# Two SBUF slots 1088 instead of 1032 columns wide: the same program at other addresses

## The chip, the cores and the metric

The kernel runs on one core of a Trainium2 chip. The metric is the device time of one execution in microseconds, taken as the median of three runs. A profile is one further execution with the hardware profiler on. Five engines work side by side and wait for each other by semaphores: PE (TensorE, the matmuls; its weight loads stand in rows of their own as PEld), DVE (VectorE), ACT (ScalarE), POOL (GpSimd) and SP (SyncE), which here issues nearly all DMAs.

## The reference

Two decoder layers over 1024 tokens of 1024 features, all in float32. What is computed, cut to its products:

```python
# layer 0: mLSTM, 8 heads, in chunks
q, k, v, o, ig, fg = split(rmsnorm(x) @ w_in)          # 1024 -> 512, 512, 1024, 1024, 8, 8
h = mlstm(q, k, v, ig, fg)                              # chunk by chunk: scores, values, carried state
x = x + rmsnorm((headnorm(h) * sigmoid(o)) @ w_out)
x = x + rmsnorm(conv_ffn(rmsnorm(x)))                   # in both layers
# layer 1: attention with a forget gate, 16 heads, K and V projected once
k, v, f = split(rmsnorm(x) @ kv_w);  q, g = split(rmsnorm(x) @ w_qg)
x = x + rmsnorm((attend(q, k, v, cumsum(logsigmoid(f))) * sigmoid(g)) @ w_out)

def conv_ffn(h):                                        # D_FF = 2816
    y = causal_conv3(h @ w_up)                          # 1024 -> 2 * 2816
    gate, val = split(y)
    return (gelu(gate) * val) @ w_down                  # 2816 -> 1024
```

## The kernel before

**Precision.** A product of two float32 matrices is made of three passes in a faster type (`fp32r`): each operand is split into a high part and a rest, and high x high, high x rest and rest x high are summed in PSUM. Line 196 (ACT) writes the high part, line 197 (DVE) the rest. So each product takes three matmuls, and PE carries almost all of the time.

**What a matmul reads.** `matmul(out, st, mv)` loads the stationary operand `st` (128 columns) into the array and streams the moving operand `mv` (512 or 256 columns) past it. Both lie in SBUF. A row of the profile for line 779 reads `b<-x,s`: the output is a PSUM bank `b`, the moving operand lies in `x`, the stationary one in a slot `s`.

**Where the operands lie.** `x` is one SBUF tile of 64 KB per partition with the split activations. All else lies in numbered slots of one pool (`Core.slot`, below), as a rule 1024 float32 columns (4096 bytes per partition) wide, or in pairs of slots that share one tile of 2048 columns: `p0` to `p5` (`PAIRS`). A few slots are wider (`WIDE`): six hold up to 4 x 272 columns of weights, and slots 2 and 31 hold 8 x 129 columns (the values of eight heads with a column of ones, the carried state). The pool lays the tiles one behind the other in the order of their first use, and `x` and the constants behind them. The mLSTM stage uses the same slots by other numbers (`renamed`).

**The stages, in order.** The mLSTM layer (until 522 us in the profile): projections of v (line 282, 256 or 272 moving columns, `gi` 0 to 3 are four column blocks), of k and q (line 282 by way of `proj_T`, 512 columns, four pairs `p` of heads each), of the gate o (256 columns), the recurrence, and the output projection (line 301). Then the first FFN: the up projection (line 779, 522 to 975 us) and the down projection (line 933, to 1188 us). Then the attention layer (to 1900 us; its projections lines 282, 1167 and 1183, scores line 1319, values line 1346, output line 301), and the second FFN (up to 2352 us, down to the end).

**The up projection** forms 22 blocks `f`. Each `f` has seven products (Strassen-like sums of blocks), and each product is 12 matmuls of 512 columns in one uninterrupted run: 84 matmuls per `f`. The moving operand of the products 11, 12, S3 and 22 is `x`, that of S2, S1 and S4 a pair of tiles `p`. The stationary weights lie here (`RIGHT` maps products to these):

```python
UP = {"11": ((18, 0), (18, 512)), "21": ((0, 0), (0, 512)), "T2": ((1, 0), (2, 0)), "T1": ((1, 512), (2, 512)),
      "T3": ((3, 0), (4, 0)), "T4": ((3, 512), (4, 512)), "22": ((5, 0), (5, 512))}
```

So product 11 takes slot 18, product 12 slot 0, S2 and S1 slots 1 and 2, S3 and 22 slots 3 and 4, S4 slot 5. In the profile a run of `b<-x,s` x36 is product 22 of one `f` with 11 and 12 of the next, x24 of `b<-p,s` is S2 and S1, then come x12 for S3 and x12 for S4.

**The down projection** copies both operands, split, into `x`, and multiplies out of `x` alone.

**The other places that the prediction names.** In the mLSTM stage, q of pairs p = 0, 1 has its weights in slots 0, 27, 1, 30, q of pairs 2, 3 in halves of `p3` and `p4`, k of pairs 2, 3 in slots 14, 32 and `p5`. Of the 256-column products, v of `gi` 3 has its (moving) weights in slots 0, 1, 27, 30, and the first o block in slots 14, 32 and `p5`.

The order of the work is the program's. In PE's long stretches it is written out by hand. It does not depend on how wide a slot is.

Of the kernel before, what the change touches and what calls it, by code (L numbers as in the profile page):

```python
# [34 lines left out]
SLACK = 0, 20  # L35
PIECES = {5: (8, 20, 26, 32, 38), 10: (6, 8, 17, 21, 25, 29, 33, 37, 41, 45)}

WIDE = {0: 1088, 1: 1088, 15: 1088, 27: 1088, 29: 1088, 30: 1088, 2: 1032, 31: 1032}
PAIRS = (19, 22), (20, 21), (23, 24), (25, 12), (26, 13), (28, 17)
PAIR = {i: (j, n) for j, two in enumerate(PAIRS) for n, i in enumerate(two)}  # L40
BLOCK = {(0, 0): 0, (0, 1): 1, (1, 1): 2, (1, 0): 3}
# [7 lines left out]
class Core:  # L49
# [30 lines left out]
    def slot(self, i, dt):  # L80
# [3 lines left out]
        if self.slots.get(key, (None, None))[1] != dt:  # L84
            n, name = (WIDE.get(i, 1024), key) if half is None else (2048, f"p{key}")
            self.slots[key] = self.arena.tile([P, n], dt, tag=name, name=name), dt
# [1499 lines left out]
```

## Time and profile before

| | us |
|---|---|
| median of three runs (2573.05 to 2577.49) | 2576.5 |
| profiled execution, its own time | 2575.71 |
| span of the profile, first to last instruction | 2574.0 |
| PE busy | 2465.4 |
| DVE busy | 1571.4 |
| ACT busy | 1167.4 |
| POOL busy | 639.6 |

The span is 1.7 us shorter than the execution's time. Matmuls overlap: a row's mean of one is how long a matmul is under way, not how often one starts. The pace of PE is read from starts: the start of one run of matmuls to the start of the next, divided by the matmuls between. All paces here were read at a granted clock of 1.00 (2.4 GHz).

### The profile page before, as it was taken

How to read it: one execution, taken by the hardware profiler on the slowest of the kernel's cores; microseconds unless marked ns; L12 is line 12 of the kernel's file. 1: busy time of each engine (PE TensorE's matmuls, PEld its weight loads, DVE VectorE, ACT ScalarE, POOL GpSimd, SP SyncE). 2: the span in 40 equal slices, each digit the busy share in tenths (PEclk: the TensorE clock that was granted, in tenths of full speed). 3: DMA queues.
4: the chain of work that ended last, by engine and by line, in shares of the span. 5: the costliest groups of instructions: out<-in, count | busy, mean ns of one | idle time of the engine just before them, and what ended most of it. 6: DMA issues, size and time to landing. Idle time of an engine off the chain costs nothing. (4 is left out here: it accounts for less than half of the span.)

```text
span 2574.0 us, 34090 instructions
## 1 busy us (share of the span) xinstructions
PE 2465.4 (96%) x12552; PEld 2047.9 (80%) x12552; DVE 1571.4 (61%) x2442; ACT 1167.4 (45%) x2078; POOL 639.6 (25%) x545
## 2 busy tenths in 40 slices
PE   7999996989999999998999999999989999999998
PEld 7988785867888888877888888887767888888886
DVE  6312544666766769558465555556776676678746
ACT  5212333344544554347255555555434454454434
POOL 0000110034454441001133333223023545442000
PEclk9999997999999999999999999999999999999999
DMA  7434333223233247443655544553332323327443
GB/s 217 117 115 139 101 90 103 90 74 106 90 115 101 88 146 263 140 140 125 195 145 137 162 132 142 156 141 119 111 102 82 103 88 116 100 90 277 144 130 128
DMA packets 291795, 332.04 MB, mean 129 GB/s; under 512 B 21036, under 2 KB 208268, under 8 KB 291628
## 3 DMA queue, kind: packets, MB, share of 16 engines
q1 hardware_dynamic: 291052, 328.82, 41.1%
q8 instruction: 98, 1.61, 0.3%
q10 hardware_dynamic: 576, 1.05, 0.1%
q14 instruction: 69, 0.57, 0.1%
HBM read 230.03 MB, written 99.78 MB: 128 GB/s over the span
## 5 line engine op out<-in xcount | busy, mean ns | idle before, releaser
L779 PE MATMUL b<-x,s 128*128 128x512 f32 x2112 | 510.8, 396 | 9.9 <-ACT s L196 5.0
L779 PEld LDWEIGHTS b<-x,s 128*128 128x128 f32 x2112 | 397.6, 189 | 107.8 <-ACT s L196 5.8
L196 ACT CAST s<-s 128x1024 fp32r<-128x1024 f32 (+3 forms) x319 | 230.5, 728 | 423.2 <-PE b L779 350.5
L197 DVE TENSOR_TENSOR s<-s,s 128x512 fp32r<-128x512 f32 (+3 forms) x312 | 282.0, 908 | 209.1 <-ACT s L196 203.6
L779 PE MATMUL b<-p,s 128*128 128x512 f32 x1584 | 389.6, 400 | 10.5 <-ACT s L787 10.4
L779 PEld LDWEIGHTS b<-p,s 128*128 128x128 f32 x1584 | 301.9, 191 | 83.9 <-ACT s L787 12.1
L933 PE MATMUL b<-x 128*128 128x512 f32 x1452 | 336.0, 389 | 1.5 <-DVE x L197 1.5
L933 PEld LDWEIGHTS b<-x 128*128 128x128 f32 x1452 | 272.4, 188 | 59.0 <-DVE x L197 2.4
L796 DVE SCALAR_TENSOR_TENSOR s<-s,cp,s 128x1023 f32<-128x1023 f32 (+1 forms) x176 | 241.0, 1372 | 28.4 <-ACT s L794 26.7
L1167 PE MATMUL b<-x,s 128*128 128x512 f32 x816 | 240.1, 411 | 0.0
L196 ACT CAST x<-s 128x1024 fp32r<-128x1024 f32 (+2 forms) x144 | 128.6, 918 | 230.8 <-PE b L933 176.9
L197 DVE TENSOR_TENSOR x<-s,x 128x1024 fp32r<-128x1024 f32 (+2 forms) x144 | 152.2, 1078 | 118.4 <-ACT x L196 117.7
L1326 POOL TENSOR_SCALAR p<-p,ring 128x256 f32<-128x256 f32 (+7 forms) x128 | 99.6, 781 | 318.4 <-DVE ring L1325 304.1
L757 POOL TENSOR_TENSOR s<-s,s 128x512 f32<-128x512 f32 x44 | 91.2, 2072 | 321.5 <-issue 198.0
L1167 PEld LDWEIGHTS b<-x,s 128*128 128x128 f32 x816 | 148.1, 190 | 24.2
L785 DVE TENSOR_TENSOR s<-s,b 128x512 f32<-128x512 f32 x132 | 90.3, 684 | 111.5 <-PE b L779 111.5
L754 POOL TENSOR_TENSOR s<-s,s 128x512 f32<-128x512 f32 x44 | 59.7, 1357 | 361.5 <-DVE ring L189 225.0
L794 ACT ACTIVATE s<-s,cp 128x1024 f32<-128x1024 f32 x88 | 109.4, 1246 | 32.0 <-DVE s L785 13.4
L197 DVE TENSOR_TENSOR p<-b,p 128x512 fp32r<-128x512 f32 x162 | 91.1, 580 | 49.5 <-ACT p L196 49.1
L196 ACT CAST p<-b 128x512 fp32r<-128x512 f32 (+2 forms) x178 | 87.9, 511 | 68.9 <-PE b L1334 46.3
L787 ACT COPY s<-b 128x512 f32<-128x512 f32 x176 | 102.3, 581 | 34.4 <-PE b L779 32.9
L282 PE MATMUL two<-s,x 128*128 128x256 f32 (+1 forms) x768 | 107.9, 289 | 10.0 <-DVE F L1131 7.8
(282 smaller groups left out, 4005.5 us busy)
## 6 DMA issues: line engine op xcount, KB each, us to landing
s<-in_ffn_w_up_dram SPq DMA_DIRECT2D x176, 256.0 KB, 3.3
s<-act SPq DMA_DIRECT2D x70, 512.0 KB, 3.9
act<-s SPq DMA_DIRECT2D x110, 256.0 KB, 2.1
s<-in_mlstm_w_in_dram SPq DMA_DIRECT2D x24, 512.0 KB, 6.6
act<-s SPq DMA_DIRECT2D x22, 512.0 KB, 2.7
s<-in_ffn_w_down_dram SPq DMA_DIRECT2D x20, 512.0 KB, 5.1
p<-in_ffn_w_down_dram SPq DMA_DIRECT2D x20, 512.0 KB, 8.0
x<-s SPq DMA_DIRECT2D x19, 512.0 KB, 2.6
```

Of the source, the lines that this page charges most:

```text
L196: self.nc.scalar.copy(hi, src)
L197: self.nc.vector.tensor_tensor(lo, src, hi, ALU.subtract)
L282: self.nc.tensor.matmul(out, st, mv, start=i == 0, stop=i == n - 1)
L757: nc.gpsimd.tensor_tensor(b21, b21, t2, ALU.subtract)
L779: nc.tensor.matmul(out, w[a][:, d], mv, start=first and d == 0 and i == 0, stop=d == 3 and i == 2, skip_group_check=True)
L785: nc.vector.tensor_tensor(out, out, bank, ALU.add)
L787: nc.scalar.copy(out, bank)
L794: nc.scalar.activation(y, u, AF.Identity, bias=cp[:, 3, col:col + 1], scale=cp[:, 2, col:col + 1])
L796: nc.vector.scalar_tensor_tensor(y[:, j:], u[:, :S - j], cp[:, 2 - j, col:col + 1], y[:, j:], ALU.mult, ALU.add)
L933: self.nc.tensor.matmul(self.banks(i)[m], st[:, p, cs], mv[:, p], start=i in (0, 1, 3) and g == p == e == 0, stop=g == self.NG - 1 and p = ...
L1167: nc.tensor.matmul(ps, st[d], k.xs(mv, d, c, 512), start=d == 0 and i == 0, stop=d == ND - 1 and i == 2)
L1326: nc.gpsimd.tensor_scalar(pt[:, :n], pt[:, :n], rd, 1.0, ALU.mult, ALU.mult)
```

## The change

One line: slots 2 and 31 get 1088 columns in place of 1032. Nothing reads or writes the new columns.

```diff
-WIDE = {0: 1088, 1: 1088, 15: 1088, 27: 1088, 29: 1088, 30: 1088, 2: 1032, 31: 1032}
+WIDE = {0: 1088, 1: 1088, 15: 1088, 27: 1088, 29: 1088, 30: 1088, 2: 1088, 31: 1088}
```

1024 columns are 16 x 256 bytes and 1088 are 17 x 256, but 1032 are 16 x 256 + 32. Every tile behind slot 31 therefore moves up by 224 bytes, and every one behind slot 2 by 448. Every engine's instructions and their order are the same in both programs, and so are all waits; only SBUF addresses differ. Remainder of a tile's first byte by 256, in the built programs (the offsets inside a tile that the large matmuls use are multiples of 256 bytes in all but the 272-column blocks):

| tiles | before | after |
|---|---|---|
| slots 0, 1, 5, 10, 11, 15, 16, 27, 29, 30, 31 and p1 | 128 | 128 |
| slots 2, 3, 4, 6, 7, 8, 18 and p0, p2, p3, p4 | 160 | 128 |
| slots 9, 14, 32 and p5, and x | 192 | 128 |

## Rows read from the trace of the kernel before

**Rows 1.** The page: span, and PE's busy time, share and instructions.
```profile
span 2574.0 us, 34090 instructions
PE 2465.4 (96%) x12552; PEld 2047.9 (80%) x12552; DVE 1571.4 (61%) x2442; ACT 1167.4 (45%) x2078; POOL 639.6 (25%) x545
```

**Rows 2.** Busy time by stage: window, length, each engine (instructions), clock, DMA share, GB/s.
```profile
620.00:975.00 355.00, 355.00 (x1531) 286.99 (x1531) 242.10 (x240) 176.46 (x221) 159.77 (x103) 1.00 0.35 115
975.00:1188.00 213.00, 210.68 (x926) 173.16 (x925) 148.63 (x176) 102.66 (x139) 13.60 (x7) 1.00 0.47 158
1255.00:1800.00 545.00, 539.11 (x3114) 450.89 (x3114) 315.31 (x643) 283.21 (x659) 174.10 (x176) 1.00 0.52 147
```

**Rows 3.** Waits of PE, the largest: total us, times, longest us.
```profile
PE b L578 <- DVE x L197: 14.9, 1, 14.9
```

**Rows 4.** Costliest groups: xcount | busy us, mean ns | idle before, releaser.
```profile
L779 PE MATMUL b<-x,s 128*128 128x512 f32 x2112 | 510.8, 396 | 9.9 <-ACT s L196 5.0
...
L779 PE MATMUL b<-p,s 128*128 128x512 f32 x1584 | 389.6, 400 | 10.5 <-ACT s L787 10.4
L933 PE MATMUL b<-x 128*128 128x512 f32 x1452 | 336.0, 389 | 1.5 <-DVE x L197 1.5
```

**Rows 5.** PE's timeline in the first up projection: start, length, group, xcount.
```profile
699.74 8.49 PE L779 MATMUL b<-x,s 128*128 128x512 f32 x36
708.07 5.75 PE L779 MATMUL b<-p,s 128*128 128x512 f32 x24
713.66 2.96 PE L779 MATMUL b<-x,s 128*128 128x512 f32 x12
716.46 2.94 PE L779 MATMUL b<-p,s 128*128 128x512 f32 x12
719.24 8.49 PE L779 MATMUL b<-x,s 128*128 128x512 f32 x36
```

**Rows 6.** The same x36, windows that begin with products 11 and 12.
```profile
702.54 2.73 PE L779 MATMUL b<-x,s 128*128 128x512 f32 x11
...
705.33 2.91 PE L779 MATMUL b<-x,s 128*128 128x512 f32 x12
```

**Rows 7.** PE's timeline, q of the mLSTM, then the first matmul of o.
```profile
177.04 5.66 PE L282 MATMUL two<-x,s 128*128 128x512 f32 x24
182.53 11.15 PE L282 MATMUL b<-x,s 128*128 128x512 f32 x48
...
211.96 5.76 PE L282 MATMUL two<-x,p 128*128 128x512 f32 x24
217.56 0.28 PE L282 MATMUL b<-s,x 128*128 128x256 f32 x1
```

**Rows 8.** PE's timeline, k of pair 2: first and last of 26 starts.
```profile
152.66 0.61 PE L282 MATMUL b<-x,s 128*128 128x512 f32 x2
...
158.56 0.40 PE L282 MATMUL b<-x,p 128*128 128x512 f32 x1
```

**Rows 9.** PE's timeline, 256 columns: v of gi 3; first row after o block 0.
```profile
115.49 2.88 PE L282 MATMUL two<-s,x 128*128 128x256 f32 x24
118.21 5.61 PE L282 MATMUL b<-s,x 128*128 128x256 f32 x48
...
240.59 2.90 PE L282 MATMUL two<-s,x 128*128 128x256 f32 x24
```

**Rows 10.** The chain that ended last, down projection: start, length, group, xcount.
```profile
2443.41 2.72 PE two L933 x12
2446.13 2.72 PE b L933 x12
```

**Rows 11.** PE's timeline, long runs of the other large matmuls.
```profile
1362.15 5.53 PE L1167 MATMUL b<-x,s 128*128 128x512 f32 x23
...
1627.48 5.33 PE L1183 MATMUL b<-s,x 128*128 128x256 f32 x44
...
1812.57 8.52 PE L301 MATMUL two<-s,x 128*128 128x512 f32 x36
```

## The prediction, made before the changed kernel had run

> **What bounds the kernel now.** I read the page's first lines, then the busy time by stage, then PE's waits. PE is busy for 2465.4 of 2574.0 us, 96% of the span [rows 1]. By stage: in the first up projection from 620 to 975 us PE has no idle time at all while DVE is busy for 242 of the 355 us, ACT for 176 and POOL for 160; the down projection and the attention layer leave PE idle for 2.3 and 5.9 us [rows 2]. The largest wait of PE in the program is 14.9 us in the mLSTM recurrence [rows 3], and the 3696 matmuls of line 779 have 20 us of idle time before them together [rows 4]. So time is lost or won only where PE's own pace changes, that is in the time from one matmul's start to the next. The other engines have some 30% of slack where PE works without a break.
>
> **What the change can touch.** It adds no instruction, moves none, and adds no wait. What is left is where operands start. I looked for PE's pace against the remainders by 256 bytes of the two operands (moving / stationary, from the table of the change).
>
> Products of 512 columns. q of pairs 2 and 3, weights at 160 and x at 192: 24 matmuls from 211.96 to 217.56 us, 233.3 ns each. q of pairs 0 and 1, weights at 128: 24 from 177.04 to 182.53, 228.8 ns. k of pair 2, weights at 192 like x: 26 from 152.66 to 158.56, 226.9 ns [rows 7, 8]. One loop, one shape, the same x; only the slots differ. The down projection takes both operands out of x, so their remainders are equal: 12 in 2.72 us, 226.7 ns [rows 10].
>
> The up projection, one f: product 22 (slots 3 and 4 at 160, x at 192) takes 2.80 us for 12, 233.3 ns; product 11 (slot 18 at 160) 2.79 us, 232.5 ns; product 12 (slot 0 at 128) 2.74 us, 228.3 ns; S2 and S1 5.59 us for 24, 232.9 ns; S3 233.3 ns; S4 231.7 ns. Together 84 in 19.50 us, 232.1 ns [rows 5, 6]. Here too the slot at 32 bytes off a multiple of 64 is the slow one, in the same run with the same engines beside it.
>
> Products of 256 columns go the other way. The first o block, all weights at 192 as x: 8 x 24 = 192 matmuls from 217.56 to 240.59 us, 120.0 ns. v of gi 3, weights at 128: 24 from 115.49 to 118.21, 113.3 ns [rows 7, 9]. So equal remainders are the best case seen at 512 columns and the worst at 256. The two prices are alike: 233.3 - 226.7 is 6.6 ns and 120.0 - 113.3 is 6.7 ns, as if a matmul either loses one step of that size or does not.
>
> The Trainium skill, page "SBUF — State Buffer", section "Who interferes with whom", gives PE two independent read ports, one for the moving operand and one for weight loads, and says that PE never waits on anyone. By that rule where a slot lies costs PE nothing and the sum below would be 0. The rows of this case (228.8 against 233.3 ns with nothing changed but the slots) do not agree with it.
>
> **The sum.** After the change every tile starts at 128, and every pair is an equal one. No row shows an undisturbed stretch in which both lie at 128, so each term goes by the equal pairs at 192 and is bounded from both sides.
>
> 1. Up projection, moving x: 2112 matmuls [rows 4], four products of seven at (233.3 + 232.5 + 228.3 + 233.3) / 4 = 231.9 ns now. Equal: 226.9 ns (k). I take 227: 4.9 ns x 2112 = -10.3 us. Bounds: -11.0 at the down projection's 226.7, +3.0 at 233.3.
> 2. Up projection, moving p: 1584, now (2 x 232.9 + 231.7) / 3 = 232.5 ns. Here the 512 columns are two pieces of 256 out of one tile, and a long equal run of that form stands nowhere. Between 226.7 (down) and 232.5 (no gain) I take the middle, 229.6: -4.6 us. Bounds: -9.2 and +1.3.
> 3. k and q: 384 matmuls. 192 at 233.3 go to 227, -1.2 us; 96 at 228.8, -0.2; the rest are equal already. -1.4 us; bounds -1.6 and +1.1 (all at 233.3).
> 4. Output projections: 768 (2 layers x 8 tiles x 8 x 3 x 2). The run of 36 takes 8.52 us; less one matmul's 0.40 that is 232.0 ns [rows 11]. These runs are cut up by transposes, and k of pair 2 also began slower than it went on, so I take half of the way to 227: 2.5 ns, -1.9 us. Bounds -4.1 and +1.0.
> 5. Attention, line 1167: 1152 (24 projections x 48). The run of 23 takes 5.53 us: less one matmul's 0.40, (5.53 - 0.40) / 22 = 233.2 ns [rows 11]. Most runs there are shorter and lie between scores and transposes; again half, 3.1 ns, -3.6 us. Bounds -7.5 and +0.1.
> 6. 256 columns, now unequal. v of gi 3: 192 x 6.7 = +1.3 us. o block 1, same slots, 24 in 2.90 us, (2.90 - 0.28) / 23 = 113.9 ns [rows 9]: 192 x 6.1 = +1.2. Line 1183, 384: (5.33 - 0.28) / 43 = 117.4 ns [rows 11]: x 2.6 = +1.0. The other 768 unequal ones lie at 160 or mixed; I give them 1.7 ns, two thirds of line 1183's loss: +1.3. Together +4.8 us. Bounds: if at 128 what counts is the moving operand's own place and not the pair, they all run at 113.3: at most 6.7 ns x 384 (gi 2, o block 0) + 4.1 x 1152 = -7.3 us; and +7 us at 120.0 for all.
> 7. Scores and values of the attention (lines 1319 and 1346, 768 matmuls in runs of two to four): too short to settle; 0, within 2.5 ns x 768 = 1.9 us either way.
> 8. The down projection: 1848 matmuls at 226.7, equal before and after: 0. If 128 behaved otherwise than 192, +6.6 ns x 1848 = 12.2 us.
> 9. DVE, ACT, POOL and DMA: their operands move too. What hides them is PE's unbroken work; in the up projection DVE could get 40% slower (355 / 242) before PE waited, and the DMA engines are busy for 35% there [rows 2]. 0; if PE gains 2% that cover stays. At PE's small waits outside, within 2 us either way.
>
> Sum of the values: -10.3 - 4.6 - 1.4 - 1.9 - 3.6 + 4.8 = -17.0 us. 2575.7 of the profiled execution becomes 2558.7; the median of the runs shown lies 0.8 us above that execution, so 2559.5, about 2560.
>
> **Rivals.**
>
> A second effect helps too: what counts for 256 columns is the moving operand's own start. Then term 6 is -7.3 instead of +4.8, and terms 1 to 5 go near their better ends (-11.0 - 7 - 1.6 - 3 - 5 = -27.6): 2576.5 - 35 = 2542. For it: the slots at 128 are the fast ones at 256 columns, and were among the faster ones at 512. Against: at 512 columns it was the stationary operand's slot that varied while x stayed, which speaks for the pair. Chance 0.12.
>
> Nothing measurable: the pace belongs to the place of a product in its loop, not to addresses, or mixed runs never settle. Terms 1 to 5 then bring 0 to 6 us, term 6 takes back up to 4.8: 2571 to 2580, say 2575. For it: S4 and S2/S1, with several remainders mixed, differ by little (231.7 and 232.9). Against: q and k differ within one loop. Chance 0.19.
>
> Slower: equal remainders are the bad case, and the down projection is fast for another reason (both operands in one tile). Then each matmul pays the step that the first o block shows: 512 columns at 233.3, in the up projection +1.2 ns x 3696 = 4.4 us, 256 columns +4.8, terms 3 to 5 +2.2; and if x at 128 loses what x at 192 had, the down projection +12.2. 2576.5 + 11 to 24, say 2598 with most of the down projection's loss. It decides from the point at which more than two in three of the 512-column matmuls lose the step. For it: 256 columns, where equal is slow, are half of 512. Against: k of pair 2, equal but in two tiles, and fast at 512. Chance 0.10.
>
> **How the numbers follow.** Forecast 0.59, the helping rival 0.12, nothing 0.19, slower 0.10. The forecast's own range is 2551 to 2570: below, terms 2, 4 and 5 at their better ends (9 us); above, term 2 at 0 and term 1 at 228.8 ns (8 us) with a little of the rest. For 8 in 10 it goes down to 2542, to the helping case's own time, and up to 2579, over nearly all of the case of nothing. About 0.2%, 5 us, is what a measurement of this kernel can tell from no change: faster means under 2571.3, slower over 2581.7. Faster: 0.58 of the forecast, 0.12 and 0.03 of the case of nothing, 0.73. Slower: 0.10 and 0.01. Same: 0.16.
>
> **What would show it.** In the profile after, one f of the up projection takes 84 x (4 x 227 + 3 x 229.6) / 7 = 19.16 us in place of 19.50, product 11's 12 matmuls 2.72 us in place of 2.79, k and q alike 227 ns, the first o block still 120.0 ns and v of gi 3 120 instead of 113.3, the down projection 2.72 us for 12, and PE's waits as they were. The forecast is wrong if product 11 still takes 2.79 us (nothing), if the down projection's twelve take 2.80 (slower), or if v of gi 3 stays at 113.3 (the helping case).

## The result, and the profile after

The changed kernel takes 2558.7 us (median of 6 runs, 2554.97 to 2560.28), the kernel before 2575.4 us on the same chip (6 runs, 2573.05 to 2578.12): the ratio is 0.9932, with a 95% interval of 0.9919 to 0.9945. That is faster by 0.7%, against a forecast of 2560 us. The profiled execution took 2559.43 us. Its first two lines on the page, to be held against [rows 1]:

```profile
span 2557.3 us, 34090 instructions
PE 2446.9 (96%) x12552; PEld 2052.2 (80%) x12552; DVE 1561.9 (61%) x2442; ACT 1163.7 (46%) x2078; POOL 650.6 (25%) x545
```

The same instructions in a span that is 16.7 us shorter. PE's busy time falls by 18.5 us, and PE is still the engine that has no slack. PE's timeline after, for a part of v (gi 3 from 109.53 us), of q (pairs 2 and 3) and one f of the up projection (columns: start us, length us, engine, line, group, count):

```profile
109.53 3.04 PE L282 MATMUL two<-s,x 128*128 128x256 f32 x24
112.41 5.92 PE L282 MATMUL b<-s,x 128*128 128x256 f32 x48
...
202.44 11.04 PE L282 MATMUL b<-x,p 128*128 128x512 f32 x48
213.32 2.88 PE L282 MATMUL two<-x,p 128*128 128x512 f32 x12
...
706.97 5.60 PE L779 MATMUL b<-p,s 128*128 128x512 f32 x24
712.41 2.88 PE L779 MATMUL b<-x,s 128*128 128x512 f32 x12
715.13 2.88 PE L779 MATMUL b<-p,s 128*128 128x512 f32 x12
717.85 8.32 PE L779 MATMUL b<-x,s 128*128 128x512 f32 x36
726.01 5.96 PE L779 MATMUL b<-p,s 128*128 128x512 f32 x24
```

Read it from start to start. One f, from 706.97 to 726.01 us, is 84 matmuls in 19.04 us, 226.7 ns each; before it took 19.50 [rows 5]. All seven products have the same pace now: 5.44 us for the 24 of S2 and S1, 2.72 for the 12 of S3 and of S4, 8.16 for the 36 of 22, 11 and 12. q with weights in pairs of slots: 48 in 10.88 us, 226.7 ns, where 24 took 5.60 us before, 233.3 ns each [rows 7]. At 256 columns it went the other way: v of gi 3 starts one every 120.0 ns (2.88 us for 24), before 113.3 [rows 9].

Busy time of the changed kernel by stretch: the one of [rows 2], then the long stretch of its first and second up projection, up to the start of its last matmul (columns as in [rows 2]):

```profile
620.00:975.00 355.00, 354.23 (x1559) 291.58 (x1558) 244.64 (x245) 177.67 (x224) 166.09 (x104) 1.00 0.36 120
...
555.07:969.97 414.90, 408.43 (x1777) 334.96 (x1776) 279.53 (x277) 203.71 (x257) 190.15 (x120) 0.99 0.34 112
...
1923.16:2335.53 412.37, 406.48 (x1777) 334.36 (x1776) 277.66 (x277) 203.58 (x257) 190.72 (x120) 0.99 0.34 112
```

And the same two up projections of the kernel before:

```profile
554.05:975.21 421.16, 415.77 (x1778) 335.09 (x1776) 283.43 (x277) 205.93 (x257) 184.33 (x120) 0.99 0.34 110
...
1930.68:2352.19 421.51, 416.43 (x1777) 335.87 (x1776) 283.17 (x277) 205.89 (x257) 184.97 (x120) 0.99 0.34 110
```

Within the same 355 us PE now starts 1559 matmuls instead of 1531, almost without idle time in either kernel. So the second up projection gives 9.1 us and the first 6.3. What of the faster pace came back can be a wait or a stretch at the lower granted clock. The changed kernel's list of waits has (waiting group, what it waits for: total us, times, longest us):

```profile
PE b L578 <- DVE x L197: 14.7, 1, 14.7
PE b L779 <- ACT s L787: 11.1, 4, 4.0
...
PE b L779 <- DVE s L785: 1.0, 2, 0.6
```

ACT s L787 was 10.4 us in [rows 4], and the wait for L785 on DVE is new; a wait for L197 on DVE fell from 1.8 to 0.2 us, so that the list's waits before line 779 come to 20.5 us after and 20.3 before. From the starts, which also show a slow start behind a wait, the first up projection loses 12.1 us against an even pace after and 9.1 before. Of this 3.2 and 2.1 us are matmuls that start only every 427 ns, at a granted clock of 0.50 (1.2 GHz), and 8.9 and 6.9 us are waits. In the second up projection the low clock takes 2.0 us after and 3.1 before, the waits 7.7 and 6.3. So the two halves differ mainly by the clock that was granted in these two executions. The largest wait of the program is as it was [rows 3]. The down projection, from the changed kernel's chain that ended last, is unchanged against [rows 10]:

```profile
2432.20 2.72 PE two L933 x12
2434.92 2.72 PE b L933 x12
```

### The profile page after: what moved, and what is told of

Read it like the earlier page. It is cut to its first block, busy times and chain, and to the rows that moved or that the text cites. A ratio compares the mean times of both kernels' runs of the same rounds, so it can differ in the third digit from the quotient of the medians.

```text
span 2557.3 us, 34090 instructions
## 1 busy us (share of the span) xinstructions
PE 2446.9 (96%) x12552; PEld 2052.2 (80%) x12552; DVE 1561.9 (61%) x2442; ACT 1163.7 (46%) x2078; POOL 650.6 (25%) x545
## 5 line engine op out<-in xcount | busy, mean ns | idle before, releaser
L779 PE MATMUL b<-x,s 128*128 128x512 f32 x2112 | 502.1, 393 | 8.5 <-ACT s L196 5.1
L779 PEld LDWEIGHTS b<-x,s 128*128 128x128 f32 x2112 | 399.9, 190 | 95.4 <-ACT s L196 5.9
L779 PE MATMUL b<-p,s 128*128 128x512 f32 x1584 | 382.6, 395 | 12.3 <-ACT s L787 11.1
L197 DVE TENSOR_TENSOR s<-s,s 128x512 fp32r<-128x512 f32 (+3 forms) x312 | 271.3, 874 | 197.7 <-ACT s L196 192.5
L1167 PE MATMUL b<-x,s 128*128 128x512 f32 x816 | 238.7, 409 | 0.0
L197 DVE TENSOR_TENSOR x<-s,x 128x1024 fp32r<-128x1024 f32 (+2 forms) x144 | 153.9, 1090 | 115.8 <-ACT x L196 115.5
L1167 PEld LDWEIGHTS b<-x,s 128*128 128x128 f32 x816 | 148.1, 190 | 22.9
L785 DVE TENSOR_TENSOR s<-s,b 128x512 f32<-128x512 f32 x132 | 90.3, 684 | 101.3 <-PE b L779 101.3
L197 DVE TENSOR_TENSOR p<-b,p 128x512 fp32r<-128x512 f32 x162 | 91.1, 580 | 48.7 <-ACT p L196 48.3
L787 ACT COPY s<-b 128x512 f32<-128x512 f32 x176 | 101.8, 579 | 26.0 <-PE b L779 25.5
```

Of the source, the lines that this page charges most:

```text
L197: self.nc.vector.tensor_tensor(lo, src, hi, ALU.subtract)
L779: nc.tensor.matmul(out, w[a][:, d], mv, start=first and d == 0 and i == 0, stop=d == 3 and i == 2, skip_group_check=True)
L785: nc.vector.tensor_tensor(out, out, bank, ALU.add)
L787: nc.scalar.copy(out, bank)
L1167: nc.tensor.matmul(ps, st[d], k.xs(mv, d, c, 512), start=d == 0 and i == 0, stop=d == ND - 1 and i == 2)
```

## The experiments

Three theories were held against each other. *Pair*: what counts is the distance between the starts of the moving and the stationary operand, by the remainder of 256 bytes. *Place*: it is each operand's own remainder (128 good, 160 bad). *Count*: each displaced tile costs its own share, so that half of the change brings half of the gain. A product below is written moving/stationary, as 192/160.

### e1_pace: the matmuls alone

The kernel is only matmuls of the model's type and shape out of two tiles, 64 to a group, without waits; the model is left out. The distance of the stationary from the moving operand grows by 32 bytes from group to group, then both are shifted together, at 512 columns and then at 256. The calls that set the groups (cut to these, with remarks added):

```diff
+for shift in range(0, 128, 8): group(512, 0, shift)      # distance, in columns of 4 bytes
+for both in range(0, 64, 8):   group(512, both, both)    # both shifted together
+for shift in range(0, 128, 8): group(256, 0, shift)
+for both in range(0, 64, 8):   group(256, both, both)
```

> Not the model: matmuls alone, 64 to a group, one moving and one stationary tile that start alike, nothing else running; first 512 columns with the stationary operand shifted by 0, 32, ... 480 bytes, then both shifted together by 0 to 224, then the same with 256 columns. Pair theory (only the distance between the two starts counts): at 512 columns 226.7 ns at 0, about 233 at 32 and 224, 228 to 230 at 64 and 192, the same again from 256 on; both shifted together 226.7 everywhere. At 256 columns 120.0 at 0, 117 to 119 at 32 and 224, 113.3 at 64 or 192. Place theory (an operand that starts 32 bytes off a multiple of 64 is slow by itself): the groups shifted together by 32, 96, 160, 224 take 233.

It ran once, in 595.4 us. PE's timeline (columns as above); 39.43 is distance 0, 53.95 is 32 bytes, 128.60 is 192, 143.27 is 224; at 306.01 both are shifted by 64; 393.25 is distance 0 at 256 columns, 408.48 is 64:

```profile
39.43 14.68 PE L36 MATMUL pc<-mv,st 128*128 128x512 f32 x64
53.95 15.09 PE L36 MATMUL pd<-mv,st 128*128 128x512 f32 x64
68.87 15.10 PE L36 MATMUL pe<-mv,st 128*128 128x512 f32 x64
...
128.60 14.83 PE L36 MATMUL pa<-mv,st 128*128 128x512 f32 x64
143.27 15.09 PE L36 MATMUL pb<-mv,st 128*128 128x512 f32 x64
...
306.01 14.70 PE L36 MATMUL pe<-mv,st 128*128 128x512 f32 x64
320.55 14.70 PE L36 MATMUL pf<-mv,st 128*128 128x512 f32 x64
...
393.25 7.83 PE L36 MATMUL pc<-mv,st 128*128 128x256 f32 x64
400.92 7.73 PE L36 MATMUL pd<-mv,st 128*128 128x256 f32 x64
408.48 7.70 PE L36 MATMUL pe<-mv,st 128*128 128x256 f32 x64
416.02 7.67 PE L36 MATMUL pf<-mv,st 128*128 128x256 f32 x64
```

(53.95 - 39.43) / 64 is 226.9 ns, (68.87 - 53.95) / 64 is 233.1, (143.27 - 128.60) / 64 is 229.2. Read from the single starts, the paces are:

| distance, bytes | 0 | 32 | 64 | 96 | 128 | 160 | 192 | 224 |
|---|---|---|---|---|---|---|---|---|
| 512 columns, ns | 226.7 | 233.3 | 233.4 | 234.1 | 232.4 | 233.3 | 229.1 | 233.3 |
| 256 columns, ns | 119.8 | 118.3 | 117.8 | 117.3 | 118.5 | 119.8 | 117.8 | 116.7 |

From 256 bytes on, the row repeats. With both operands shifted together a group's mean stays between 226.8 and 227.2 ns at all eight places (119.8 at 256 columns), and 226.7 from its eighth matmul on. So the place alone does nothing, and the distance sets the pace without any other engine at work. Two expectations failed: the 113.3 ns at 256 columns did not show, the lowest here is 116.7; and a distance of 64 bytes gives 233.4 at 512 columns, not 228 to 230.

### e2_all32: everything equal, elsewhere

The changed kernel with one small tile ahead of all others, so that every tile starts at 160 in place of 128.

```diff
+ahead = ctx.enter_context(tc.tile_pool(name="ahead", bufs=1))
+nc.gpsimd.memset(ahead.tile([P, 8], F32, name="ahead"), 0.0)
```

> The changed kernel with everything 32 bytes further on, all slots and x at 160. Pair theory: no difference to the changed kernel, 2555 to 2562 us, up projection 226.7 ns a matmul. Place theory: every large matmul has both operands 32 off a multiple of 64: up and down projections at 233, 5544 x 6.6 ns = 37 us more, about 2595 us.

2559.5 us (5 runs, 2558.38 to 2563.28), 0.9938 [0.9924, 0.9951] of the kernel before. Its timeline, products 22, 11 and 12:

```profile
699.63 8.32 PE L781 MATMUL b<-x,s 128*128 128x512 f32 x36
707.79 5.60 PE L781 MATMUL b<-p,s 128*128 128x512 f32 x24
```

36 in 8.16 us, 226.7 ns, at the very remainder that looked like the slow one before. The place theory falls in the model as well.

### e3_only31: half of the change

```diff
-WIDE = {..., 2: 1032, 31: 1032}
+WIDE = {..., 2: 1032, 31: 1088}
```

Now x, p5 and the slots 9, 14 and 32 lie at 160, the rest at 128: only a few tiles are displaced, but x is one of them, and nearly all its partners are elsewhere.

> Half of the change: slot 31 widened, slot 2 not; slots before slot 2's end at 128, slots 9, 14, 32, p5 and x at 160. Pair theory: x is now 32 off nearly every slot: products 11, 12, S3, 22 at 233 (2112 x 6.5 = 14 us more than the changed kernel), S4 mixed at 231 (2 us), k, q, output and line 1167 6 us more, 256 columns 2 us less: about 2579 us, slower than the kernel before, though more tiles are at 128 than there. If it is enough that slots lie at 128 whatever x does: 2560 us.

2578.9 us (11 runs, 2573.62 to 2580.46), 1.0006 [0.9997, 1.0015]: no gain. One f in the timeline, 22 with 11 and 12, then S2 with S1, then S3:

```profile
699.97 8.56 PE L779 MATMUL b<-x,s 128*128 128x512 f32 x36
708.36 5.64 PE L779 MATMUL b<-p,s 128*128 128x512 f32 x24
713.84 2.97 PE L779 MATMUL b<-x,s 128*128 128x512 f32 x12
```

The products out of x (160/128) take 8.39 / 36 = 233.1 ns. S2 and S1 out of p (128/128) come to 5.48 / 24 = 228.3 ns: equal pairs, but S2, which follows the slow run, has eight starts of 229 to 235 ns before it settles (229.9 on average), and only S1 behind it runs at 226.7. What p gains (3.2 us over the trace against the kernel before), x and the 256-column products lose (2.8 and 3.4 us).

### e5_only2: the other half

```diff
-WIDE = {..., 2: 1032, 31: 1032}
+WIDE = {..., 2: 1088, 31: 1032}
```

Here x and most slots lie at 160; the slots 0, 1, 5, 10 and 11 and p1 lie at 128.

> The other half of the change: slot 2 widened, slot 31 not; x, p0, p2 to p5 and slots 2, 3, 4, 18 at 160, slots 0, 1, 5, 10, 11 and p1 still at 128. Pair theory: products 11, S3 and 22 become equal pairs (160), but 12 and S4 are 32 off and S2 and S1 mixed; an equal run behind an unequal one starts slowly: the first three about 228.5, 12 at 233, p products 231 to 233: 14 us more than the changed kernel in the up projections, 3 us elsewhere, about 2576 us, no gain over the kernel before. If each half of the change were worth half of the gain: 2567 us.

2569.5 us (8 runs, 2564.82 to 2572.47), 0.9973 [0.9963, 0.9984]. I expected 2576 and was wrong by 6.5 us. The timeline, the same products:

```profile
699.93 8.41 PE L779 MATMUL b<-x,s 128*128 128x512 f32 x36
708.18 5.76 PE L779 MATMUL b<-p,s 128*128 128x512 f32 x24
713.78 2.89 PE L779 MATMUL b<-x,s 128*128 128x512 f32 x12
716.51 2.95 PE L779 MATMUL b<-p,s 128*128 128x512 f32 x12
```

22, 11 and 12 take 8.25 us: 11 and 22 (160/160) run at 227.0 ns, 12 (160/128) at 233.3. S3 (160/160) takes 2.73 / 12 = 227.5, although slow products stand on either side of it. I had given such runs 228.5 and more to settle. S2 and S1 (160/128 for the most part) stay at 5.60 / 24 = 233.3. So the two halves bring +2.1 us (e3, its interval holds no change) and -6.6 us by their medians; together they would make -4.5 and not -16.7. The count theory falls: what counts is how many matmuls have an equal pair.

### e4_x64: x alone moved

The changed kernel with 64 bytes ahead of x: all slots at 128, x at 192.

```diff
+nc.gpsimd.memset(c.tile([P, 16], F32, name="ahead"), 0.0)
 self.x = c.tile([P, 16384], F32R, name="x")
```

> The changed kernel with x alone 64 bytes further on (192, slots at 128). Pair theory: products with x at 229.3 ns (2112 x 2.5 = 5 us more), p products unchanged at 226.8, the down projection unchanged, other 512-column products 3 to 4 us more; 256 columns 113.3 in place of 120.0, up to 1536 x 6.6 = 10 us less, of which the recurrence hides some: 2555 to 2562 us, no clear difference to the changed kernel. Place theory (64-byte starts are enough): everything as in the changed kernel, 256 columns at 120.0.

2565.7 us (5 runs, 2560.44 to 2568.46), 0.9957 [0.9944, 0.997]. From the timeline, 22 with 11 and 12, then S2 with S1:

```profile
698.81 8.42 PE L780 MATMUL b<-x,s 128*128 128x512 f32 x36
707.07 5.65 PE L780 MATMUL b<-p,s 128*128 128x512 f32 x24
712.56 2.93 PE L780 MATMUL b<-x,s 128*128 128x512 f32 x12
```

The products of x (192/128) take 8.26 / 36 = 229.4 ns, as at distance 192 alone (229.1). The output projections have x as the stationary operand: 128/192, distance 64, and run at 233.5 ns, as the matmuls alone at 64 (233.4). The sign of the distance counts. The 256-column products of line 282 come down to 114.7 ns, lower than e1 shows at any distance (116.7). S2 and S1, with an equal pair, take 5.49 / 24 = 228.8 ns: S2, behind products of x, has ten starts of 224 to 236 ns, and S1 runs at 226.7.

The time lies above the 2555 to 2562 us that were expected. Against the changed kernel, by the starts over each trace, the products of x take 5.0 us more, as expected, and the other 512-column products 5.0 in place of 3 to 4; those of p take 1.8 us more where none was expected, and the 256-column ones give back 5.3 of the up to 10 that were expected. Together this is 6.5 of the 6.7 us by which the two spans differ.

### e6_pace_passes: the matmuls alone, in the model's order

As e1 (the model is left out again), but in the order of three passes, 72 to a group; then groups of 12 that alternate between distance 0 and 32; then steps of 8 bytes, 48 to a group. The lines that differ from e1, shortened:

```diff
-m = 64 + moved + 512 * (i % 4); s = 64 + shift + 128 * (i % 16)
+d, e = divmod(i, 3)
+m = 64 + 1024 * (e == 1) + n * (d % 2); s = 64 + shift + 1024 * (e == 2) + P * (d % 4)
+for _ in range(8): group(512, 0, 12); group(512, 8, 12)
+for shift in range(0, 64, 2): group(512, shift, 48)
```

> Not the model: matmuls alone, in the order of the three passes (same weights twice, then the rests). 512 then 256 columns with the stationary operand shifted by 0, 32, ... 224; then runs of 12 that alternate between equal and 32 bytes off, then 36 equal and 12 off, then 72 equal; then 512 columns with shifts in steps of 8 bytes. Pair theory: 512 as in e1_pace (226.7, 233, 233, 234, 232, 233, 229, 233); 256: 120.0 at 0 and 113.3 at 64 as in the model. An equal run behind one that was off begins at 230 to 236 and settles at 226.7 within 10 to 15 matmuls, so equal runs of 12 average about 230. Steps of 8 bytes: only 0 reaches 226.7. If each matmul were on its own: equal runs of 12 at 226.7 from the first.

It ran once, in 724.1 us. At 512 columns the table above comes out again within 0.1 ns, at 256 columns within 0.2 but for distance 224 (117.9). In the timeline 247.22 is a group of 12 at distance 32, 250.02 one at 0 and 252.75 one at 32 again; of the steps of 8 bytes, 359.77 is 8, and 516.26 is 120:

```profile
247.22 2.96 PE L37 MATMUL pd<-mv,st 128*128 128x512 f32 x12
250.02 2.89 PE L37 MATMUL pe<-mv,st 128*128 128x512 f32 x12
252.75 2.96 PE L37 MATMUL pf<-mv,st 128*128 128x512 f32 x12
...
359.77 11.24 PE L37 MATMUL pe<-mv,st 128*128 128x512 f32 x48
370.85 11.36 PE L37 MATMUL pf<-mv,st 128*128 128x512 f32 x48
...
516.26 11.05 PE L37 MATMUL pc<-mv,st 128*128 128x512 f32 x48
527.14 11.32 PE L37 MATMUL pd<-mv,st 128*128 128x512 f32 x48
```

Twelve unequal ones take 2.80 us (233.3 ns), twelve equal ones 2.73 (227.5): the first equal one takes 231 ns, the next already 226.7. So here an equal run settles after one matmul, where I had expected 10 to 15 and an average of about 230. Not every run does: the first group of 512 columns behind one of 256 needed nine, each group of e1 that shifts both operands seven, S2 in e3 eight and S2 in e4 ten. In e6's alternating groups and in S3 of e5, which settle at once, the moving operand keeps its remainder; in those of e1, e3 and e4 it changes with the run. No run changes that alone. I had also expected 0 to be the only good distance. Eight bytes cost 11.08 / 48 = 230.8 ns, but 120 bytes take 10.88 / 48 = 226.7, as good as equal. Of the 32 steps none but these two comes under 228.

### e7_shift256: the 256-column products put where they are faster

The changed kernel with the split weights of the 256-column products stored 192 bytes further into their slots, so that they lie, as moving operand, at 64 and the stationary x 64 bytes above it. All products of 512 columns stay equal. Some slots become wider for it; a few instructions of DVE, ACT and SP change places.

```diff
+SHIFT = {0, 1, 27, 30, 10, 11, 14, 32, 25, 12, 26, 13, 28, 17}
+place = self.shifted if n == 256 else self.r       # 48 columns into the slot
+hi = place(sh, nd * n)...; lo = place(sl, nd * n)...
```

> The changed kernel, with most of the 256-column weights stored 192 bytes into wider slots (p3, p4, p5 and slots 10, 11, 14, 32 wider by 256 bytes, so all tiles stay at 128): the stationary x then starts 64 bytes above the moving weights there, and every 512-column pair stays equal. A few instructions of DVE, ACT and SP change places by new overlaps. Pair theory: the v blocks (576) and the attention's v (192) at 114 to 116 in place of 120.0, 3 to 4 us less; o blocks 0 to 2 up to 3 us less where the recurrence does not hide it: 2552 to 2556 us. If equal remainders are best for everything: 2559 or more.

2555.2 us (4 runs, 2551.04 to 2556.27), 0.9915 [0.9901, 0.9928] of the kernel before. Its timeline, v of gi 3, and 22 with 11 and 12 of one f:

```profile
113.57 2.88 PE L295 MATMUL two<-s,x 128*128 128x256 f32 x24
116.29 5.60 PE L295 MATMUL b<-s,x 128*128 128x256 f32 x48
...
714.31 8.32 PE L792 MATMUL b<-x,s 128*128 128x512 f32 x36
722.47 2.88 PE L792 MATMUL b<-p,s 128*128 128x512 f32 x12
```

v of gi 3 is back at 2.72 / 24 = 113.3 ns, the 256-column products of line 282 as a whole at 116.5 (119.9 in the changed kernel), and 22 with 11 and 12 stays at 8.16 us. 1920 products of 256 columns at about 3 ns make 6 us by the paces; 2.6 us arrived against the next run. One part of the difference may be the clock, which no run tests: the mean granted clock was 0.982 to 0.985 in the four runs of e7 and 0.985 to 0.987 in the five of e8.

### e8_after_again: the changed kernel beside e7

Nothing edited: the changed kernel in the same set of runs as e5 to e7.

> The changed kernel itself, to stand beside e7_shift256 and e5_only2 on the same chip: 2557 to 2561 us.

2557.8 us (5 runs, 2556.48 to 2558.47), 0.9927 [0.9915, 0.994]. The gain repeats in a second set of runs. e7 is the best version of all, by 2.6 us over this, but the two intervals overlap, so that it isn't clearly apart from the changed kernel.

## Why the prediction was right

The step on which all rested, that an equal pair is the fast case at 512 columns and among the slowest at 256, is shown: alone in e1 and e6, at another remainder in e2, and undone in e3. The Trainium skill, page "SBUF — State Buffer", section "Who interferes with whom", calls PE's two read ports independent. If this is read as a rule that the place of a pair costs nothing, e1 disagrees, with 233.3 ns at a distance of 32 bytes against 226.7 at 0 and no other engine at work.

Two readings in the prediction's working do not hold. It is not "as if a matmul either loses one step of that size or does not": distances of 192, 8 and 128 bytes give 229.1, 230.8 and 232.4 ns. And "the slot at 32 bytes off a multiple of 64" is not slow by itself: in e2 everything lies there and runs at 226.7.

Its terms, by the time from each matmul's start to the next one's, added up over each trace (a wait behind a matmul is in its sum, and so is a stretch at the lower clock):

| term | before, us | after, us | measured | predicted |
|---|---|---|---|---|
| 1 up, moving x | 515.7 | 506.4 | -9.3 | -10.3 |
| 2 up, moving p | 375.4 | 369.7 | -5.7 | -4.6 |
| 3 k and q | 91.0 | 89.1 | -1.9 | -1.4 |
| 4 output projections | 190.6 | 187.9 | -2.7 | -1.9 |
| 5 line 1167 | 290.3 | 288.2 | -2.1 | -3.6 |
| 6 256 columns | 236.0 | 241.5 | +5.5 | +4.8 |
| 7 scores and values (384 of 512 columns) | 95.4 | 95.5 | +0.1 | 0 |
| 8 down | 427.2 | 427.1 | 0.0 | 0 |

The rows sum to -16.1 us, and the spans differ by 16.7; the other 0.6 us lie in matmuls of other lines and shapes. The single terms are off by -1.1 to +1.5 us and cancel to 0.9, so that part of the closeness of the total is luck.

- Term 1: the pace went from 232.0 to 226.8 ns, x 2112 = -11.0 us, a little better than the 227 assumed. 1.7 us of it did not arrive, and this is the clock and not a wait: 27 of these matmuls, before 14, fell into stretches at a granted clock of 0.50 and started every 427 ns (2.7 us more), while the waits fell by 0.9 us. In e8, the same program again, it was 19, so this part differs from one execution to the next.
- Term 2 was mis-sized by its pace. The form of two pieces reached 227.1 ns, not the 229.6 chosen between the bounds: (232.3 - 227.1) x 1584 is -8.2 us, near the better bound of -9.2. 2.5 us of it was lost again in waits (27 and 26 of these matmuls at the low clock). So two errors, of the pace and of "PE's waits as they were" (term 9), partly cancel within this term.
- Terms 3 to 5: the projections of L301 reach 228.7 ns and those of L1167 231.5, for which 229.5 and 230.1 were assumed. Term 5 was mis-sized the most, by 1.5 us: the pace gained 1.8 ns (from 233.4), not 3.1. The trace shows where the rest stays (a run of L1167, and its part from the eleventh matmul on):

```profile
1427.42 5.28 PE L1167 MATMUL b<-x,p 128*128 128x512 f32 x22
...
1429.81 2.89 PE L1167 MATMUL b<-x,p 128*128 128x512 f32 x12
1432.54 0.27 PE L1334 MATMUL b<-ident,p 128*128 128x128 f32 x1
```

  The first ten of this run take 2.39 us, the other twelve 2.73. Over all runs of L1167, starts under 300 ns apart average 231.7 ns within a run's first ten matmuls (233.0 before) and 226.7 from the eleventh on (232.2 before); 955 of the 1152 are among the first ten. So behind matmuls of another shape an equal pair gains 1.3 ns at first and 5.5 only from about the eleventh on. The 233.2 ns of the prediction came from a run whose first two starts lie 320 ns apart; without that gap it went at 229.4, and that 233.2 is near the 233.4 of the whole line is luck.
- Term 6: v of gi 3 stands at 120.0 ns as forecast, the group as a whole went from 117.6 to 119.9. Of the 4.9 us in line 282 some 3.5 are pace (2.3 x 1536). The rest is 16 matmuls that started every 213 ns, where the clock was 0.50; the gaps are as before (6.8 and 6.9 us). That stretch stands behind a wait of 2.0 us, which the kernel before has too, without a fall of the clock (columns as in [rows 2]):

```profile
85.31:88.70 3.39, 3.39 (x19) 3.39 (x18) 2.69 (x4) 2.49 (x4) 0.00 (x0) 0.50 0.14 19
```

- Term 8: 2.72 us for 12 out of x at 128, as at 192. This fits e1, where only the distance counts: it is 0 in both.
- What was to show it: one f 19.04 us (19.16 forecast), product 11 2.72, k and q both 227, the first o block still 120.0.

The sum has one slip that changes little: at their better ends terms 2, 4 and 5 give 10.7 us more, not 9, and the lower end would be 2549.

The rivals: "helping" needed 256 columns at 113.3 with both at 128, and they stand at 120.0. "Nothing" needed product 11 at 2.79 us. "Slower" needed the down projection at 2.80. None shows.

Two things stay open. In the model the 256-column products come to 113.3 ns at a distance of 64 (v of gi 3 in e7), alone they never come under 116.7, in either order of e1 and e6; something of the model's loop that these leave out must matter. And what in the chip makes the step, and why 120 bytes are as good as 0, no run shows.

## What to carry to other kernels

Where PE works without a break, read its pace from start to start for each pair of tiles, not for each line, and sort it by the remainders of both addresses: a loop whose pace varies with nothing but the slot is the sign. Then pad the tiles so that all operands of the large matmuls start alike, and do it for all of them: of the two halves of this padding the one that left x displaced gained nothing, and the other 6.6 of the 16.7 us. Expect the full gain in long runs only: behind matmuls of another shape a run needed up to ten matmuls to reach its pace. Measure narrow matmuls apart, since at 256 columns the order of good and bad is another one.

## What the runs showed of the hardware that was not expected

- A matmul of 512 columns (fp32r, with a weight load to each) starts at best every 226.7 ns, and every 228 to 234 ns at all but one of the other distances of its two operands that were tried; the step of up to 7 ns repeats with 256 bytes and isn't symmetric (229.1 at 192, 233.4 at 64).
- Besides equal starts, a distance of 120 bytes has the full pace (226.7 ns); 8 bytes off already cost 4 ns (230.8).
- An equal run does not always start at its pace: behind matmuls of another shape the first ten of a run of L1167 average 231.7 ns, the later ones 226.7; the groups of e1 that begin at another place need seven matmuls, those of e6 whose moving operand stays in place one.
- At 256 columns equal starts are among the slowest (119.8 ns alone, 120.0 in the model), 64 bytes give 117.8 alone and down to 113.3 in the model.
- The step is there only at the full granted clock. In stretches with a granted clock of 0.50 (1.2 GHz), such as the first matmuls of the up projection, both kernels start one of 512 columns every 426.7 ns, which is 512 cycles at 1.2 GHz, with unequal pairs before and equal ones after.
